# Sixteen-fold positions and remainders written by ScalarE for the routing of a product-key expert layer

## The chip, the cores and the metric

The kernel runs on one core of a Trainium2 chip. The metric is the device time of one execution in microseconds (us); a kernel's time is the median of its runs. The engines are named as the profile names them: PE (TensorE, the matmuls) and PEld (its weight loads), DVE (VectorE), ACT (ScalarE), POOL (GpSimd), SP (the DMA-issuing SyncE).

## The reference

Two layers, each a mixer (attention, convolution and a gated scan) and a channel mixer called PEER, on 512 tokens of width 1024. The change lies in PEER alone:

```python
s1 = jnp.einsum('thd,nd->thn', q[:, :, 0], keys1).astype(jnp.float32)
s2 = jnp.einsum('thd,nd->thn', q[:, :, 1], keys2).astype(jnp.float32)
v1, i1 = lax.top_k(s1, PEER_TOPK)
v2, i2 = lax.top_k(s2, PEER_TOPK)
cand = (v1[..., :, None] + v2[..., None, :]).reshape(T, PEER_HEADS, PEER_TOPK * PEER_TOPK)
sc, ci = lax.top_k(cand, PEER_TOPK)
e1 = jnp.take_along_axis(i1, ci // PEER_TOPK, axis=-1)
e2 = jnp.take_along_axis(i2, ci % PEER_TOPK, axis=-1)
experts = (e1 * PEER_NKEYS + e2).reshape(T, hk)
gates = jax.nn.softmax(sc, axis=-1).reshape(T, hk).astype(xn.dtype)
```

Each token has 8 heads of 16 winners, 128 experts in all; of each expert the layer uses one row of `u` (with a Gelu behind it) and one row of `v`, weighted by the gate.

## The kernel before

Tokens lie in four blocks of 128 (one token to a partition). Three blocks are computed densely: for each of 128 chunks of 128 experts, `hidden` (L639) multiplies the chunk of `u` with the 384 tokens into a PSUM tile `psh` of which there are two; ScalarE makes Gelu of it into `ht` (L645). A chunk of `u` is split in two parts first: ScalarE casts it to `uh` (L630), VectorE subtracts to get `ul` (L631), three buffers each; the matmuls of a chunk need both. For the first 72 chunks `ht` goes to memory as `H` by a DMA that ScalarE's own queue issues (L769). The gates are spread into a dense matrix `G` by `gate_matrix` (L952): four one-hot operations on VectorE for every 16 tokens, matmuls into `psg`, ScalarE copies them to `stg` (L976), and ScalarE's queue issues the DMA to `G` (L977). The fourth block is computed by gathering rows with indirect DMAs (`gathered`, L719), one VectorE step a row; `tick` hands out these steps.

What fills the gate matrix comes from `route` (L878), which runs four times a layer in the order block 0, block 3 (the gathered one), block 1, block 2: "first" to "fourth route" below. It forms 50 candidate sums a head (`cand`), finds the 16 largest and their positions `si` (`top16`), makes the softmax of the gates (an Exp on ScalarE, L898), and then turns a position into a pair of keys. For that it compares each of 128 positions with the 16 starts of the candidate groups (L923, 128x2048 elements of 16 bits), multiplies the result with two tables (L925, L926), sums over the 16 (`total`, L920 and L921), takes the remainder `bi` (L930), compares it with 0 to 15 (L932), multiplies (L933) and sums again. Three transposes on TensorE (`rtr`, L943 to L945) end the first, third and fourth route. In both comparisons the position or remainder is read through `bc(..., [[1, HK], [0, 16]])`: the innermost step of that operand is 0. The tiles `ge`, `pr`, `ci`, `bi` have one buffer each.

The order of the work isn't written out by hand. The program's order gives priorities, and a planner places each instruction on its engine's queue as soon as it takes its inputs to be ready, except where `pin` keeps the order. Each engine then runs its queue in order. A loop over 75 steps (L762) traces one chunk a step, and beside it as much of `route` and `gate_matrix` as keeps the sum of the numbers that their `yield` statements hand out at or below 2.72 a step (L772); rows are gathered from the end of the second route on, 0.8 a step.

Of the kernel before, what the change touches and what calls it, by code (L numbers as in the profile page):

```python
# [10 lines left out]
F16 = mybir.dt.float16  # L11
# [3 lines left out]
OP = mybir.AluOpType  # L15
# [4 lines left out]
P = 128  # L20
# [6 lines left out]
NH = 8  # L27
NK = 16
# [31 lines left out]
def bc(ap, pattern):  # L60
    return bass.AP(tensor=ap.tensor, offset=ap.offset, ap=[ap.ap[0]] + pattern)


class K:
# [813 lines left out]
    def route(self, V12, I12, rp, gate, hk=None, tb=0, idx=None, base=0):  # L878
        nc = self.nc
        cand = rp.tile([P, NH, NCAND], F32, tag="cand", name="cand")  # L880
        v1, v2 = V12[:, 0], V12[:, 1]
        for a in range(5):
            s, n = GRP_START[a], GRP_LEN[a]
            nc.vector.tensor_tensor(cand[:, :, s:s + n], v2[:, :, 0:n], bc(v1[:, :, a:a + 1], [[NK, NH], [0, n]]), op=OP.add)
        s = GRP_START[5]
        nc.vector.tensor_tensor(cand[:, :, s:s + 6].rearrange("p h (a b) -> p h a b", b=2),
                                bc(v1[:, :, 5:8], [[NK, NH], [1, 3], [0, 2]]),
                                bc(v2[:, :, 0:2], [[NK, NH], [0, 3], [1, 2]]), op=OP.add)
        s = GRP_START[8]
        nc.vector.tensor_tensor(cand[:, :, s:s + 8], v1[:, :, 8:16], bc(v2[:, :, 0:1], [[NK, NH], [0, 8]]), op=OP.add)  # L890
        sv = rp.tile([P, NH, NK], F32, tag="sv", name="sv")
        si = rp.tile([P, NH, NK], U32, tag="si", name="si")
        for h in range(NH):
            self.top16(cand[:, h], sv[:, h], si[:, h])
            yield 0.65
        gt = gate.rearrange("p (h k) -> p h k", h=NH)
        nc.vector.tensor_tensor(gt, sv, bc(sv[:, :, 0:1], [[NK, NH], [0, NK]]), op=OP.subtract)
        nc.scalar.activation(gt, gt, AF.Exp)  # L898
        zs = rp.tile([P, NH], F32, tag="zs", name="zs")
        nc.vector.tensor_reduce(zs, gt, axis=AX.X, op=OP.add)  # L900
        nc.vector.reciprocal(zs, zs)
        nc.vector.tensor_tensor(gt, gt, bc(zs, [[1, NH], [0, NK]]), op=OP.mult)

        ci = rp.tile([P, NH, NK], F16, tag="ci", name="ci")
        nc.vector.tensor_copy(ci, si)
        ii = rp.tile([P, 2, NH, NK], F16, tag="ii", name="ii")
        nc.vector.tensor_copy(ii, I12)
        d1 = rp.tile([P, NH, NK], F16, tag="d1", name="d1")
        nc.vector.tensor_copy(d1[:, :, 0:1], ii[:, 0, :, 0:1])
        nc.vector.tensor_tensor(d1[:, :, 1:NK], ii[:, 0, :, 1:NK], ii[:, 0, :, 0:NK - 1], op=OP.subtract)  # L910
        HK = NH * NK
        ge = rp.tile([P, HK, 16], F16, tag="ge", name="ge")
        pr = rp.tile([P, 2, HK, 16], F16, tag="pr", name="pr")
        ex = rp.tile([P, 3, HK], F32, tag="ex", name="ex")
        cib = bc(ci, [[1, HK], [0, 16]])
        yield 2.0

        def total(n, dst):
            for w in (8, 4, 2):
                nc.vector.tensor_tensor(pr[:, 0:n, :, 0:w], pr[:, 0:n, :, 0:w], pr[:, 0:n, :, w:2 * w], op=OP.add)  # L920
            nc.vector.tensor_tensor(dst, pr[:, 0:n, :, 0], pr[:, 0:n, :, 1], op=OP.add)  # L921

        nc.vector.tensor_tensor(ge, cib, bc(self.starts, [[0, HK], [1, 16]]), op=OP.is_ge)  # L923
        hv = lambda t: t.rearrange("p (h k) j -> p h k j", h=NH)
        nc.vector.tensor_tensor(hv(pr[:, 0]), hv(ge), bc(d1, [[NK, NH], [0, NK], [1, 16]]), op=OP.mult)  # L925
        nc.vector.tensor_tensor(pr[:, 1], ge, bc(self.dstart, [[0, HK], [1, 16]]), op=OP.mult)  # L926
        yield 4.6
        total(2, ex[:, 0:2])
        bi = rp.tile([P, HK], F16, tag="bi", name="bi")
        nc.vector.tensor_tensor(bi, ci.rearrange("p h k -> p (h k)"), ex[:, 1], op=OP.subtract)  # L930
        yield 2.6
        nc.vector.tensor_tensor(ge, bc(bi, [[1, HK], [0, 16]]), bc(self.iota16, [[0, HK], [1, 16]]), op=OP.is_equal)  # L932
        nc.vector.tensor_tensor(hv(pr[:, 0]), hv(ge), bc(ii[:, 1], [[NK, NH], [0, NK], [1, 16]]), op=OP.mult)  # L933
        total(1, ex[:, 1:2])
        yield 4.6

        if idx is not None:
            nc.vector.tensor_scalar(ex[:, 0], ex[:, 0], float(NCH), float(base), op0=OP.mult, op1=OP.add)
            nc.vector.tensor_tensor(idx, ex[:, 0], ex[:, 1], op=OP.add)
            return  # L940
        E1, E2, GH, GL = hk
        tr = self.psC.tile([P, 3, P], F32, tag="c", name="rtr2")
        nc.tensor.transpose(tr[:, 0], ex[:, 0], self.ident)  # L943
        nc.tensor.transpose(tr[:, 1], ex[:, 1], self.ident)
        nc.tensor.transpose(tr[:, 2], gate, self.ident)  # L945
        s = slice(tb * P, tb * P + P)
        nc.scalar.copy(E1[:, s], tr[:, 0])
        nc.scalar.copy(E2[:, s], tr[:, 1])
        nc.scalar.activation(GH[:, s], tr[:, 2], AF.Copy, scale=GSCALE)
        nc.vector.scalar_tensor_tensor(GL[:, s], tr[:, 2], GSCALE, GH[:, s], op0=OP.mult, op1=OP.subtract)  # L950
# [97 lines left out]
```

## Time and profile before

| | |
|---|---|
| three runs, median (lowest to highest) | 3073.7 us (3073.36 to 3074.85) |
| the profiled execution | 3068.26 us, of which the span is 3066.5 us |
| granted TensorE clock, mean of the span | 0.994 |

The span runs from the first to the last instruction of the profile; 1.8 us lie around it. The page's busy times are shares of that span. An engine's idle time matters only where the engine that the end waits for stood still with it, so the page is read together with the timeline of single waits.

### The profile page before, as it was taken

The numbers are of one execution on the slowest core, as the hardware profiler recorded it, in microseconds if no ns is written. First come the engines' busy times: TensorE is split into PE (matmuls) and PEld (weight loads), VectorE is DVE, ScalarE is ACT, GpSimd is POOL, SyncE is SP. The second block draws the span as 40 slices with busy tenths as digits, with TensorE's granted clock in tenths as the row PEclk, the third lists the DMA queues.
The fourth block names the chain that finished last, engine by engine and source line by source line (L and its number), as shares of the span: only waits on it lengthen the run. The fifth ranks groups of instructions, "written<-read, shape, count | busy, mean of one in ns | idle before, by whom it ended". The sixth has DMA issues, their size and how long they took to land.

```text
span 3066.5 us, 45595 instructions
## 1 busy us (share of the span) xinstructions
PE 2996.6 (98%) x16742; PEld 2657.9 (87%) x16742; DVE 2470.3 (81%) x5079; ACT 1268.5 (41%) x1874; POOL 739.7 (24%) x543
## 2 busy tenths in 40 slices
PE   8999999999999999999999999999999999999998
PEld 7777889999999998788878788899998999988886
DVE  5777999987778887877766769999878877878777
ACT  5244346556333333333352433465553333323333
POOL 0000000222455544322100000002225555543221
PEclk9999999999999999999999999999999999999999
DMA  4112238799998888999722122478999888889996
GB/s 123 56 45 91 89 122 263 260 316 334 338 333 324 322 325 307 357 338 334 275 76 69 59 72 90 155 246 287 310 343 340 321 326 331 331 306 350 334 344 232
DMA packets 335664, 757.03 MB, mean 247 GB/s; under 512 B 30000, under 2 KB 192208, under 8 KB 331344
## 3 DMA queue, kind: packets, MB, share of 16 engines
q1 hardware_dynamic: 141904, 407.00, 37.1%
q0 software_dynamic: 73728, 268.47, 24.5%
q10 hardware_dynamic: 119808, 78.66, 8.2%
q8 instruction: 131, 2.15, 0.3%
q14 instruction: 93, 0.76, 0.1%
HBM read 673.28 MB, written 80.74 MB: 246 GB/s over the span
## 4 chain that ended last, share of the span: by engine, by line
PE 74%; issue 7%; DVE 7%; POOL 4%; DMA 3%; ACT 3%; ACTq 1%; SPq 0%; POOLq 0%; DVEq 0%
PE pv L77 9%; PE pv L75 9%; PE pv L76 9%; PE psh L75 8%; PE psh L77 8%; PE psh L76 8%; POOL row L715 4%; PE psp L77 2%; PE psp L76 2%; PE psp L75 2%; DMA row<-in_v_rows,idx 2%; PE psq L76 2%; PE psq L77 2%; PE psq L75 2%; PE pst L545 1%
## 5 line engine op out<-in xcount | busy, mean ns | idle before, releaser
L715 POOL DMA_INDIRECT row<-in_u_rows,idx x256 | 390.6, 1526 | 1315.9 <-DVE si L873 669.5
L75 PE MATMUL psh<-ahi,uh 128*128 128x384 f32 x2048 | 694.7, 339 | 10.3 <-ACT ht L645 10.3
L77 PE MATMUL psh<-ahi,ul 128*128 128x384 f32 x2048 | 689.6, 337 | 6.6 <-DVE ul L631 6.6
L76 PE MATMUL psh<-alo,uh 128*128 128x384 f32 x2048 | 688.8, 336 | 0.0
L75 PE MATMUL pv<-vh,wh 128*128 128x512 f32 x1536 | 598.1, 390 | 8.1 <-ACT wh L815 8.1
L77 PE MATMUL pv<-vh,wl 128*128 128x512 f32 x1536 | 601.2, 392 | 0.0
L76 PE MATMUL pv<-vl,wh 128*128 128x512 f32 x1536 | 600.3, 391 | 0.0
L715 POOL DMA_INDIRECT row<-in_v_rows,idx x256 | 331.5, 1295 | 601.5 <-DVE yacc L732 565.7
L630 ACT CAST uh<-uraw 128x1024 fp32r<-128x1024 f32 x288 | 302.5, 1053 | 322.0 <-PE psh L76 156.1
L631 DVE TENSOR_TENSOR ul<-uraw,uh 128x1024 fp32r<-128x1024 f32 x288 | 350.4, 1220 | 99.3 <-ACT uh L630 87.9
L75 PEld LDWEIGHTS psh<-ahi,uh 128*128 128x128 f32 x2048 | 387.0, 189 | 16.4 <-ACT ht L645 12.2
L77 PEld LDWEIGHTS psh<-ahi,ul 128*128 128x128 f32 x2048 | 386.8, 189 | 7.2 <-DVE ul L631 7.2
L76 PEld LDWEIGHTS psh<-alo,uh 128*128 128x128 f32 x2048 | 387.3, 189 | 4.1
L801 DVE TENSOR_TENSOR vl<-vraw,vh 128x1024 fp32r<-128x1024 f32 x256 | 312.6, 1221 | 83.2 <-issue 64.5
L645 ACT ACTIVATE ht<-psh 128x384 f32<-128x384 f32 x256 | 125.3, 489 | 612.4 <-PE psh L77 605.5
L75 PEld LDWEIGHTS pv<-vh,wh 128*128 128x128 f32 x1536 | 288.7, 188 | 67.5 <-ACT wh L815 10.5
L77 PEld LDWEIGHTS pv<-vh,wl 128*128 128x128 f32 x1536 | 289.0, 188 | 62.6 <-DVE wl L801 1.9
L76 PEld LDWEIGHTS pv<-vl,wh 128*128 128x128 f32 x1536 | 289.1, 188 | 59.4 <-DVE vl L801 1.0
L732 DVE SCALAR_TENSOR_TENSOR yacc<-row,wk,yacc 128x1024 f32<-128x1024 f32 x254 | 325.7, 1282 | 10.9 <-DMA row<-in_v_rows,idx 9.3
L723 DVE SCALAR_TENSOR_TENSOR gscr<-row,xg 128x1024 f32<-128x1024 f32 x256 | 312.4, 1220 | 13.2 <-DMA row<-in_u_rows,idx 11.6
L815 ACT CAST wh<-ht 128x384 fp32r<-128x384 f32 x256 | 130.7, 510 | 385.0 <-PE pv L76 229.5
L806 ACT CAST vh<-vraw 128x1024 fp32r<-128x1024 f32 x256 | 268.7, 1050 | 25.3 <-DMA vraw<-in_v_rows 24.5
(285 smaller groups left out, 4451.2 us busy)
## 6 DMA issues: line engine op xcount, KB each, us to landing
uraw<-in_peer_u SPq DMA_DIRECT2D x256, 512.0 KB
vraw<-in_v_rows SPq DMA_DIRECT2D x256, 512.0 KB
G<-stg ACTq DMA_DIRECT2D x48, 1024.0 KB
g<-G SPq DMA_DIRECT2D x32, 1536.0 KB
H<-ht ACTq DMA_DIRECT2D x144, 192.0 KB
ht<-H SPq DMA_DIRECT2D x144, 192.0 KB
wraw<-in_w_in SPq DMA_DIRECT2D x96, 256.0 KB
uraw<-in_peer_w_q SPq DMA_DIRECT2D x32, 512.0 KB
```

Of the source, the lines that this page charges most:

```text
L75: mm(ps, ah, bh, start=first, stop=False)
L76: mm(ps, ah, bl, start=False, stop=False)
L77: mm(ps, al, bh, start=False, stop=last)
L630: pin(nc.scalar.copy(hi, src))
L631: self.last = pin(nc.vector.tensor_tensor(lo, src, hi.bitcast(F32), op=OP.subtract))
L645: pin(nc.scalar.activation(hs[c], ps, AF.Gelu))
L715: nc.gpsimd.indirect_dma_start(out=r, out_offset=None, in_=ins[name], in_offset=bass.IndirectOffsetOnAxis(ap=idx[:, k:k + 1], axis=0))
L723: nc.vector.scalar_tensor_tensor(sc, r, 1.0, xg, op0=OP.mult, op1=OP.mult, accum_out=hd[:, k:k + 1])
L732: nc.vector.scalar_tensor_tensor(yacc, r, wk[:, k:k + 1], yacc, op0=OP.mult, op1=OP.add)
L801: self.last = pin(nc.vector.tensor_tensor(lo, src, hi.bitcast(F32), op=OP.subtract))
L806: pin(nc.scalar.copy(vh[c], vs[c]))
L815: pin(nc.scalar.copy(wh[c], hs[c]))
```

## The change

ScalarE gets two more instructions a route: it copies the 128 positions, and later the 128 remainders, each sixteen times side by side, into the second half of the tile `pr` (2048 elements of 16 bits a partition). Both comparisons on VectorE then read that copy, whose innermost step is 1. The second half of `pr` is free at both places: the product with `dstart` (L926) is written into it behind the first comparison, and has been summed before the second copy. Two `yield` numbers go from 4.6 to 3.6; `ge` and `pr` are declared earlier, and `ci` gets a flat shape.

```diff
-        ci = rp.tile([P, NH, NK], F16, tag="ci", name="ci")
-        nc.vector.tensor_copy(ci, si)
+        HK = NH * NK
+        ge = rp.tile([P, HK, 16], F16, tag="ge", name="ge")
+        pr = rp.tile([P, 2, HK, 16], F16, tag="pr", name="pr")
+        wide = pr[:, 1]
+        nc.scalar.copy(wide, bc(si, [[1, HK], [0, 16]]))
+        ci = rp.tile([P, HK], F16, tag="ci", name="ci")
+        nc.vector.tensor_copy(ci, si.rearrange("p h k -> p (h k)"))
...
-        cib = bc(ci, [[1, HK], [0, 16]])
...
-        nc.vector.tensor_tensor(ge, cib, bc(self.starts, [[0, HK], [1, 16]]), op=OP.is_ge)
+        nc.vector.tensor_tensor(ge, wide, bc(self.starts, [[0, HK], [1, 16]]), op=OP.is_ge)
...
-        yield 4.6
+        yield 3.6
         total(2, ex[:, 0:2])
         bi = rp.tile([P, HK], F16, tag="bi", name="bi")
-        nc.vector.tensor_tensor(bi, ci.rearrange("p h k -> p (h k)"), ex[:, 1], op=OP.subtract)
+        nc.vector.tensor_tensor(bi, ci, ex[:, 1], op=OP.subtract)
+        nc.scalar.copy(wide, bc(bi, [[1, HK], [0, 16]]))
         yield 2.6
-        nc.vector.tensor_tensor(ge, bc(bi, [[1, HK], [0, 16]]), bc(self.iota16, [[0, HK], [1, 16]]), op=OP.is_equal)
+        nc.vector.tensor_tensor(ge, wide, bc(self.iota16, [[0, HK], [1, 16]]), op=OP.is_equal)
...
-        yield 4.6
+        yield 3.6
```

## Rows read from the trace of the kernel before

**Rows 1.** The page: the span, and each engine's busy us (share of the span, instructions).

```profile
span 3066.5 us, 45595 instructions
PE 2996.6 (98%) x16742; PEld 2657.9 (87%) x16742; DVE 2470.3 (81%) x5079; ACT 1268.5 (41%) x1874; POOL 739.7 (24%) x543
```

**Rows 2.** Busy time of each engine over the stretch in which the routing runs, once per layer. Columns: stretch, its length, then busy us (instructions) of PE, PEld, DVE, ACT, POOL, then granted clock, DMA share, GB/s.

```profile
400.00:780.00 380.00, 370.40 (x2603) 363.96 (x2602) 333.82 (x688) 212.68 (x269) 58.57 (x42) 0.99 0.81 271
1920.00:2300.00 380.00, 371.70 (x2619) 364.82 (x2618) 336.52 (x699) 214.20 (x271) 58.81 (x42) 0.99 0.81 269
```

**Rows 3.** Timeline of TensorE in those two stretches, matmuls ahead of which it stood idle (left out: waits under 0.3 us, one of 1.00 us at 428.08, and layer 1's others). Columns: start, length, engine, line, operation, out<-in, and in brackets the idle time before it and what ended it.

```profile
421.08 0.44 PE L77 MATMUL psh<-ahi,ul 128*128 128x384 f32 x1 [3.28 <-DVE ul L631]
441.96 0.33 PE L944 MATMUL rtr<-ident,ex 128*128 128x128 f32 x1 [0.31 <-DVE ex L921]
530.40 0.45 PE L75 MATMUL psh<-ahi,uh 128*128 128x384 f32 x1 [2.85 <-ACT ht L645]
765.89 0.45 PE L75 MATMUL psh<-ahi,uh 128*128 128x384 f32 x1 [1.98 <-ACT ht L645]
2052.56 0.45 PE L75 MATMUL psh<-ahi,uh 128*128 128x384 f32 x1 [2.38 <-ACT ht L645]
```

**Rows 4.** Waits of TensorE over the whole run: its two groups on psh, the tile of the hidden layer's matmuls. Columns: engine, line, what it waited for, us in total, times, longest.

```profile
PE psh L75 <- ACT ht L645: 10.3, 6, 2.8
PE psh L77 <- DVE ul L631: 6.6, 2, 3.3
```

**Rows 5.** Busy time in the 20 us around the wait at 530.40 (columns as in rows 2), for the granted clock; then, from the chain that ended last, a matmul right behind that wait and one 3 us later (start, us, what).

```profile
520.00:540.00 20.00, 17.15 (x90) 16.83 (x89) 20.00 (x48) 7.79 (x10) 1.66 (x1) 0.91 0.80 285
...
531.36 0.32 PE psh L75
534.67 0.17 PE psh L77
```

**Rows 6.** Groups of VectorE instructions by line and shape over the whole run. Columns: line, engine, operation, out<-in, shapes, count, busy us, mean ns of one, idle time before them.

```profile
L923 DVE TENSOR_TENSOR ge<-ci,starts 128x2048 f16<-128x2048 f16 x8 | 18.3, 2283 | 0.0
L932 DVE TENSOR_TENSOR ge<-bi,iota 128x2048 f16<-128x2048 f16 x8 | 18.2, 2278 | 0.0
L926 DVE TENSOR_TENSOR pr<-ge,dstart 128x2048 f16<-128x2048 f16 x8 | 9.7, 1208 | 0.0
```

**Rows 7.** The same view for ScalarE.

```profile
L630 ACT CAST uh<-uraw 128x1024 fp32r<-128x1024 f32 x288 | 302.5, 1053 | 322.0 <-PE psh L76 156.1 <-PE psq L76 82.1 <-PE psg L974 28.2
L976 ACT ACTIVATE stg<-psg 128x512 f32<-128x512 f32 x192 | 186.0, 1121 | 12.2 <-issue 9.9 <-PE psg L974 2.3
L80 ACT CAST wh<-wraw 128x512 fp32r<-128x512 f32 x96 | 57.2, 619 | 44.9 <-DMA wraw<-in_w_in 39.9 <-PE psp L76 4.4
```

**Rows 8.** Timeline of ScalarE (ACT; ACTq is its own queue issuing a DMA) and of VectorE around the third route of layer 0.

```profile
519.79 7.12 ACTq L769 DMA_DIRECT2D H<-ht  x1
526.94 1.28 ACT L898 ACT_TABLE_LOAD   x1 [6.24 <-issue]
528.23 0.31 ACT L898 ACTIVATE gt<-gt 128x128 f32<-128x128 f32 x1
529.86 0.49 ACT L645 ACTIVATE ht<-psh 128x384 f32<-128x384 f32 x1
...
523.78 2.29 DVE L923 TENSOR_TENSOR ge<-ci,starts 128x2048 f16<-128x2048 f16 x1
528.39 1.22 DVE L631 TENSOR_TENSOR ul<-uraw,uh 128x1024 fp32r<-128x1024 f32 x1
```

**Rows 9.** The same place in layer 1, ScalarE.

```profile
2042.41 6.66 ACTq L769 DMA_DIRECT2D H<-ht  x1
2052.01 0.49 ACT L645 ACTIVATE ht<-psh 128x384 f32<-128x384 f32 x1
```

**Rows 10.** First route of layer 0: timeline of ScalarE, then of VectorE.

```profile
436.19 1.05 ACT L630 CAST uh<-uraw 128x1024 fp32r<-128x1024 f32 x1 [2.38 <-PE psh L76]
...
420.94 2.29 DVE L923 TENSOR_TENSOR ge<-ci,starts 128x2048 f16<-128x2048 f16 x1
433.46 1.23 DVE L631 TENSOR_TENSOR ul<-uraw,uh 128x1024 fp32r<-128x1024 f32 x1 [0.75 <-ACT uh L630]
434.60 0.28 DVE L930 TENSOR_TENSOR bi<-ci,ex 128x128 f16<-128x128 f16 x1
434.92 2.29 DVE L932 TENSOR_TENSOR ge<-bi,iota 128x2048 f16<-128x2048 f16 x1
441.54 0.36 DVE L921 TENSOR_TENSOR ex<-pr 128x128 f32<-128x128 f16 x1
```

**Rows 11.** Fourth route of layer 0: timeline of VectorE, then of ScalarE.

```profile
579.12 0.28 DVE L930 TENSOR_TENSOR bi<-ci,ex 128x128 f16<-128x128 f16 x1
...
584.77 0.49 ACT L645 ACTIVATE ht<-psh 128x384 f32<-128x384 f32 x1
586.56 1.05 ACT L630 CAST uh<-uraw 128x1024 fp32r<-128x1024 f32 x1 [1.30 <-PE psh L76]
```

**Rows 12.** VectorE: the last read of the shared tile by the third route of layer 0, and a step of the fourth route behind its last position.

```profile
541.72 0.43 DVE L921 TENSOR_TENSOR ex<-pr 128x128 f32<-128x128 f16 x1
551.96 0.23 DVE L905 CAST ci<-si 128x128 f16<-128x128 uint32 x1
```

**Rows 13.** ScalarE in a stretch with no routing step beside it.

```profile
548.75 1.06 ACT L630 CAST uh<-uraw 128x1024 fp32r<-128x1024 f32 x1 [2.72 <-PE psh L76]
```

More of the change, by code (lines that the diff above doesn't have):

```diff
@@ L910, in route @@
         nc.vector.tensor_tensor(d1[:, :, 1:NK], ii[:, 0, :, 1:NK], ii[:, 0, :, 0:NK - 1], op=OP.subtract)
-        HK = NH * NK
-        ge = rp.tile([P, HK, 16], F16, tag="ge", name="ge")
-        pr = rp.tile([P, 2, HK, 16], F16, tag="pr", name="pr")
         ex = rp.tile([P, 3, HK], F32, tag="ex", name="ex")
-        cib = bc(ci, [[1, HK], [0, 16]])
         yield 2.0
```

## The prediction

> **What bounds the kernel now.** I read the page first: TensorE is busy for 98% of the span, VectorE for 81%, ScalarE for 41% [rows 1]. So VectorE's time is worth something only where TensorE stands still. Next the two stretches that hold the routing, one a layer: in 380 us TensorE is busy for 370.4 and 371.7 us, VectorE for 334 and 337, ScalarE for 213 and 214 [rows 2]. All that the change can win there is the rest of TensorE, 9.6 and 8.3 us, and what a lowered clock costs behind each wait. Then the waits themselves [rows 3]. Those shown of layer 0 are 3.28 us for `ul`, 0.31 us for the end of the first route, 2.85 and 1.98 us for `ht`; the reader is to see that the routing's own products end only the shortest. Summed over the run, TensorE waits on `psh` 10.3 us for ScalarE's `ht` and 6.6 us for VectorE's `ul` [rows 4]. ScalarE, the engine that gets the new work, is the one whose lateness TensorE feels more. Last the clock: in the 20 us around the wait of 2.85 us it was granted at 0.91, and right behind the wait a matmul advances the chain by 0.32 us, 3 us later by 0.17 [rows 5]: the lower of the two levels, 1.2 GHz, after idleness. 9% of 20 us is 1.8 us on top of the wait.
>
> **The change part by part.** *The comparisons.* Sixteen of them (two a route, four routes, two layers) take 2283 and 2278 ns each. The product with `dstart` has the same size and type, and the operands that the comparisons will have, one dense and one 16 values read again and again; it takes 1208 ns [rows 6]. I take that: 1.07 us less each, 17.2 us less VectorE time in all, 8.6 us a layer. On the path to the end this is worth nothing by itself: TensorE's long waits are for `ul` behind the first route's top-16 search, which ends before the first comparison (420.94) [rows 3, 10], and for `ht`. Its bounds are 0 and the 0.31 us a layer of the wait for `rtr`.
>
> *The copies.* Sixteen ScalarE instructions of 2048 elements a partition. No row has that size. The cast between the same memories takes 619 ns for 512 elements and 1053 ns for 1024 [rows 7], 434 ns for each further 512, so 1053 + 2 x 434 = 1.92 us. The strided copy into `stg` takes 1121 ns for 512 [rows 7], which would make 4 x 1121 = 4.48 us; the new copy writes densely, so I take 1.92 and keep 4.48 for the range. ScalarE gets 31 us more in all. The Trainium skill (page "ScalarE: Activation LUTs", section "What ACT_TABLE_LOAD costs") gives 186 ns plus 0.833 ns an element, an estimate of 1.89 us, which leaves the sum as it is.
>
> Away from the routing ScalarE stands idle for 2.72 us ahead of each `uh` cast [rows 13], which hides a copy of 1.92 us whole. Without that cover it would cost up to 1.92 us. Three places are tighter.
>
> *(a) Third route, first copy, both layers.* ScalarE's queue is held for 7.12 us by the issue of an `H` DMA, until 526.94, and only then runs the table load for Exp, Exp at 528.23 and, after another table load, the Gelu into `ht` at 529.86, which releases TensorE at 530.40 [rows 3, 8]. The positions of this route are ready before its first comparison at 523.78, inside the held time [rows 8]. So the copy is queued behind the DMA, beside Exp, in front of that `ht`, and TensorE's wait grows by the copy: 1.92 us. Layer 1 repeats it (6.66 us held, `ht` at 2052.01, wait of 2.38 us) [rows 3, 9]. The clock is already lowered there, so I add nothing for it. Sum 2 x 1.92 = 3.8 us; bounds 0 (queued behind `ht`) and 2 x 4.48 = 9.0.
>
> *(b) First route, second copy.* `bi` is done at 434.88; ScalarE is idle until 436.19; the copy would end at 436.8, the comparison would start 1.9 us later than its 434.92 and last 1.07 us less, so the chain to `rtr` would be 0.8 us longer and the wait at 441.96 with it [rows 3, 10]. Against it: the first comparison ends some 0.7 us earlier in the same route, and VectorE stands idle 0.75 us ahead of the subtraction at 433.46 in front of `bi` [rows 10], so `bi` can come before that subtraction. I take 0; bounds 0 and 2 x 0.8 = 1.6.
>
> *(c) Fourth route, second copy.* `bi` is ready at 579.4. `ht` ends at 585.26 and ScalarE next waits for TensorE until 586.56 [rows 11]: a margin of 1.3 us against 1.92. I take 0; bounds 0 and 2 x 0.6 = 1.2.
>
> *What waits behind a waiting instruction.* A copy that waits for `si` or `bi` holds the `uh` casts, Gelus and DMA issues queued behind it, and TensorE waits for the first two. A comparison that waits for its copy holds the `ul` subtractions and the one-hot operations behind it on VectorE. The copy must also wait until the route before has read `pr` for the last time. The third route does so by 542.15 and the fourth has its positions before 551.96 [rows 12], so this costs nothing; without that margin of nearly 10 us it would hold ScalarE for what was missing.
>
> *The `yield` numbers* fall by 8 a layer, 8 / 2.72 = 2.9 of 75 steps: routing and gate matrices get their priority that much earlier, with their DMAs into `G` on ScalarE's queue, in front of `H` DMAs that the same queue issues. The third route's numbers start at 74.8 before and 70.8 now, that is in step 28 and step 27, so 0.8 of a gathered row more is asked for in these 75 steps, and POOL issues it a step sooner. TensorE's groups of waits on `psh` name no row [rows 4]; I take 0, and the re-sorting that it may cause is in the rivals.
>
> Sum: 3.8 us. Against the profiled execution that is 3068.26 + 3.8 = 3072.1 us; the median of the runs lies 5.4 us above that execution, so I forecast 3073.7 + 3.8 = 3077.5 us.
>
> **The rivals.** *Nothing is seen (3073.7 us):* the copy is queued behind `ht` in (a) too. For it speaks that nothing in the program orders the two; against it, that Exp, whose input comes at nearly the same time, was queued in front of `ht`.
>
> *Faster (3064.9 us):* the copy pushes Exp and its two table loads behind the waiting `ht`. Then `ht` could run at 526.94 in place of 529.86 [rows 8], and the waits of 2.85 and 2.38 us and 1.8 us of clock each would go: 8.8 us. For it: a longer queue at that place is a reason for the planner to take the older `ht` first. Against it: that `ht` must look ready to the planner before Exp does, and in the trace of before it did not.
>
> *Slower (3083 us):* VectorE becomes late behind its new wait. In (a) the copy ends at 526.94 + 1.92 = 528.86 at the earliest, so the comparison starts 5.1 us later than 523.78 and, being 1.07 us shorter, ends 4.0 us later; the subtraction at 528.39 behind it moves to 532.4 and ends at 533.6 [rows 8], 1.3 us after TensorE could go on at 530.40 + 1.92. It decides once that `ul` belongs to the very next chunk. With (b) and (c) in full it is 2 x (1.92 + 1.3 + 0.8 + 0.6) = 9.2 us. Against it: three buffers of `ul`. The Trainium skill (page "ScalarE: Activation LUTs", section "Rules for kernel authors") sends simple elementwise work to VectorE rather than ScalarE, so it speaks against this change. If its exchange were all on one path, 16 x (1.92 - 1.07) = 13.6 us would be lost, 3087.3 us; ScalarE at 41% busy [rows 1] says that most of it is not.
>
> *The comparison isn't shortened (3077.5 us still):* if it stayed at 2.28 us, VectorE would lose what nothing waits for. The row of `dstart` [rows 6] speaks against it.
>
> **How the numbers follow.** Forecast 0.32, nothing seen 0.15, comparison not shortened 0.03, faster 0.22, slower 0.28. About 0.2% (6.1 us) is what a measurement of this kernel can tell from no change; the first three cases lie within it, so the same has 0.50, faster 0.22 and slower 0.28. The range goes from the faster case, rounded down to 3064, to 3084, which takes in the slower case and (a) at the dear copy (3082.7). The prices past both ends are left out.
>
> **What would show it.** After the change the two comparisons should take about 1.2 us, and sixteen ScalarE copies about 1.9 us. At the held `H` DMA of each layer the copy should stand in front of the `ht` that releases TensorE, and that wait should be 4.8 and 4.3 us. The wait for `rtr` should stay near 0.3 us. I am wrong if the waits on `ul` multiply in the routing stretches, if the held place is reordered, or if TensorE's idle time changes outside these stretches.

## The result and the profile after

The changed kernel takes 3095.39 us (median of 6 runs, 3091.6 to 3100.69), the kernel before 3074.27 us on the same chip (6 runs, 3068.8 to 3077.99): +21.1 us, a ratio of 1.0070 with a 95% interval of 1.0057 to 1.0083. That is past the upper end of the range.

The profiled execution of the changed kernel took 3100.69 us, 5.3 above its median; that of the kernel before (3068.26) lay 6.0 below the median of 3074.27. So the two profiles stand 32.4 us apart where the medians stand 21.1. Below, places are read from the profiles and sizes from the medians.

First the page, beside [rows 1], and the groups of the new and changed instructions, beside [rows 6] (count, busy us, mean ns of one, idle time before them).

```profile
span 3098.9 us, 45600 instructions
PE 3006.6 (97%) x16742; PEld 2665.2 (86%) x16742; DVE 2454.0 (79%) x5079; ACT 1295.6 (42%) x1890; POOL 746.8 (24%) x543
```

```profile
L932 ACT COPY pr<-bi 128x2048 f16<-128x2048 f16 x8 | 15.2, 1899 | 12.4 <-DVE bi L931 12.0 <-ACT ht L645 0.4
L908 ACT CAST pr<-si 128x2048 f16<-128x2048 uint32 x8 | 15.1, 1892 | 12.0 <-DVE si L876 9.6 <-issue 2.4
L924 DVE TENSOR_TENSOR ge<-pr,starts 128x2048 f16<-128x2048 f16 x8 | 9.8, 1223 | 8.6 <-ACT pr L908 8.6
L934 DVE TENSOR_TENSOR ge<-pr,iota 128x2048 f16<-128x2048 f16 x8 | 9.7, 1213 | 2.3 <-ACT pr L932 1.5 <-issue 0.8
```

The prices are those forecast: comparisons of 1.21 to 1.22 us, copies of 1.89 to 1.90 (forecast 1.92). VectorE is busy 16.3 us less, ScalarE 27.1 us more, and TensorE does the same 16742 matmuls. The time is lost in where things stand. Layer 0's routing stretch, cut at the start of chunks 0, 25, 49 and 75 of `psh`, before and after (columns as in [rows 2]):

```profile
403.81:536.24 132.43, 124.99 (x868) 122.29 (x867) 131.12 (x380) 77.16 (x96) 4.84 (x4) 0.97 0.64 210
536.24:652.15 115.91, 115.73 (x836) 114.31 (x836) 109.82 (x189) 64.25 (x82) 25.11 (x17) 1.00 0.84 283
652.15:780.08 127.93, 125.95 (x888) 124.33 (x886) 89.63 (x100) 70.67 (x90) 28.62 (x21) 0.99 0.96 327
```

```profile
405.28:532.35 127.07, 122.94 (x869) 120.65 (x867) 109.31 (x313) 79.89 (x97) 0.00 (x0) 0.99 0.65 205
532.35:662.80 130.45, 120.79 (x836) 117.11 (x836) 113.10 (x242) 76.56 (x92) 30.43 (x21) 0.97 0.83 276
662.80:796.82 134.02, 127.64 (x885) 125.08 (x885) 101.25 (x116) 69.82 (x88) 33.40 (x22) 0.97 0.92 315
```

The first third gains 5.4 us (the waits of 1.00 and 2.85 us of [rows 3] are gone), the second loses 14.5 and the third 6.1, with the clock granted at 0.97 in place of 1.00 and 0.99. VectorE did 313 instructions in the first third where it did 380: the routing has slid to the right. Layer 1's stretch, before and after:

```profile
1926.43:2299.91 373.48, 365.18 (x2586) 359.43 (x2585) 330.64 (x667) 212.10 (x268) 58.81 (x42) 0.99 0.82 272
```

```profile
1943.21:2333.71 390.50, 372.51 (x2586) 363.47 (x2585) 323.61 (x669) 226.04 (x276) 59.70 (x43) 0.98 0.80 267
```

That is 17.0 us more, and 15.3 in layer 0: together 32.3 of the 32.4 us by which the profiles differ, so next to nothing is lost outside these stretches. TensorE's waits over 1 us in layer 0's (same view as [rows 3]) are new ones, but for the 3.28 us for `ul` behind the first route's search, which stay:

```profile
558.92 0.69 PE L77 MATMUL psh<-ahi,ul 128*128 128x384 f32 x1 [5.26 <-DVE ul L631]
578.50 0.33 PE L946 MATMUL rtr<-ident,ex 128*128 128x128 f32 x1 [1.73 <-DVE ex L922]
656.42 0.44 PE L75 MATMUL psh<-ahi,uh 128*128 128x384 f32 x1 [2.15 <-ACT ht L645]
664.48 0.45 PE L75 MATMUL psh<-ahi,uh 128*128 128x384 f32 x1 [1.16 <-ACT uh L630]
781.49 0.69 PE L75 MATMUL psh<-ahi,uh 128*128 128x384 f32 x1 [4.43 <-ACT ht L645]
```

Layer 1 has the waits for `ul` (3.12 us) and for `rtr` (1.74) again; at its end two waits for `ht`, of 1.92 and 1.99 us, stand in place of the 4.43.

*The wait at 558.92.* The timelines of ScalarE (first row), VectorE and POOL around the second route:

```profile
516.29 1.89 ACT L908 CAST pr<-si 128x2048 f16<-128x2048 uint32 x1
...
518.22 1.23 DVE L924 TENSOR_TENSOR ge<-pr,starts 128x2048 f16<-128x2048 f16 x1 [2.08 <-ACT pr L908]
541.20 0.27 DVE L941 TENSOR_TENSOR idx<-ex 128x128 int32<-128x128 f32 x1
547.32 1.23 DVE L723 SCALAR_TENSOR_TENSOR gscr<-row,xg 128x1024 f32<-128x1024 f32 x1 [1.73 <-DMA row<-in_u_rows,idx]
552.91 1.23 DVE L723 SCALAR_TENSOR_TENSOR gscr<-row,xg 128x1024 f32<-128x1024 f32 x1 [3.60 <-DMA row<-in_u_rows,idx]
557.65 1.22 DVE L631 TENSOR_TENSOR ul<-uraw,uh 128x1024 fp32r<-128x1024 f32 x1
...
542.41 1.09 POOL L715 DMA_INDIRECT row<-in_u_rows,idx  x1 [360.34 <-DVE sv L875]
543.81 2.16 POOL L715 DMA_INDIRECT row<-in_u_rows,idx  x1 [0.30 <-issue]
```

The second route's first copy stands on ScalarE behind the copies into `stg` of the first route's gate matrix, though its positions were ready at 487.40, so its comparison runs at 518.22, where before it ran at 486.45, and `idx` comes at 541.20 in place of 514.67. Before, the first row step ran at 550.43, 36 us behind `idx`; now VectorE comes to it at 545.6 (547.32 less the 1.73 of waiting), 4 us behind `idx`, while the first row takes 4.9 us from its issue at 542.41. VectorE waits for two rows in turn, and `ul` with it.

*The wait at 781.49.* SyncE's queue at the end of the stretch, before and after:

```profile
758.34 0.33 SPq L627 DMA_DIRECT2D uraw<-in_peer_u  x1
768.94 0.33 SPq L791 DMA_DIRECT2D g<-G  x1
```

```profile
761.23 0.61 SPq L627 DMA_DIRECT2D uraw<-in_peer_u  x1
769.18 0.33 SPq L791 DMA_DIRECT2D g<-G  x1
769.60 1.08 SPq L627 DMA_DIRECT2D uraw<-in_peer_u  x2
...
780.00 1.04 ACT L630 CAST uh<-uraw 128x1024 fp32r<-128x1024 f32 x1 [8.58 <-DMA uraw<-in_peer_u]
```

The last stage's first load of `g` waits for the last `G` DMA. Before it was queued behind the stretch's 76th `uraw` load, now behind the 73rd, so five loads (74 to 78) stand behind that wait in place of two, and ScalarE waits 8.58 us for one.

### The profile page after: what moved, and what is told of

It is laid out like the page before. It is cut to its first block, busy times and chain, and to the rows that moved or that the text cites. A ratio compares the mean times of both kernels' runs of the same rounds, so it can differ in the third digit from the quotient of the medians.

```text
span 3098.9 us, 45600 instructions
## 1 busy us (share of the span) xinstructions
PE 3006.6 (97%) x16742; PEld 2665.2 (86%) x16742; DVE 2454.0 (79%) x5079; ACT 1295.6 (42%) x1890; POOL 746.8 (24%) x543
## 5 line engine op out<-in xcount | busy, mean ns | idle before, releaser
L77 PE MATMUL psh<-ahi,ul 128*128 128x384 f32 x2048 | 694.6, 339 | 15.3 <-DVE ul L631 15.2
L631 DVE TENSOR_TENSOR ul<-uraw,uh 128x1024 fp32r<-128x1024 f32 x288 | 350.3, 1220 | 127.0 <-ACT uh L630 115.9
L732 DVE SCALAR_TENSOR_TENSOR yacc<-row,wk,yacc 128x1024 f32<-128x1024 f32 x254 | 325.8, 1283 | 14.5 <-DMA row<-in_v_rows,idx 13.1
```

What stands on the lines that cost most here:

```text
L77: mm(ps, al, bh, start=False, stop=last)
L631: self.last = pin(nc.vector.tensor_tensor(lo, src, hi.bitcast(F32), op=OP.subtract))
L732: nc.vector.scalar_tensor_tensor(yacc, r, wk[:, k:k + 1], yacc, op0=OP.mult, op1=OP.add)
```

## The experiments

Differences are median against median of the kernel before on the same chip. "Loads behind" means that the last stage's first loads (`vraw`, `g`) are queued behind the last `uraw` of the stretch. The ratio and the two medians don't agree to the microsecond everywhere: e9's 1.0046 is 14 us, its medians give 11.6. Each interval reaches some 3 to 6 us to either side, so a difference between two rows of the table is known to about 5 us only (an estimate from these intervals).

| label | copies in routes | numbers | else | median us | against before | ratio (95% interval) |
|---|---|---|---|---|---|---|
| change | all | 3.6 | | 3095.39 | +21.1 | 1.0070 (1.0057 to 1.0083) |
| e1 | all | 3.6 | copies planned first | 3101.07 | +26.5 | 1.0087 (1.0072 to 1.0102) |
| e2 | 1, 3, 4 | 3.6 | | 3082.88 | +8.3 | 1.0029 (1.0019 to 1.0038) |
| e3 | 2 | 3.6 | | 3095.88 | +21.3 | 1.0065 (1.0049 to 1.0082) |
| e4 | none | 3.6 | | 3090.26 | +15.7 | 1.0049 (1.0036 to 1.0062) |
| e5 | none | 3.6 | loads behind | 3077.09 | +2.8 | 1.0006 (0.9997 to 1.0015) |
| e6 | none | 4.6 | loads behind | 3072.86 | -1.5 | 0.9993 (0.9982 to 1.0005) |
| e7 | all | 4.6 | | 3075.11 | +0.8 | 1.0003 (0.9991 to 1.0015) |
| e8 | all | 3.6 | loads behind | 3091.65 | +17.3 | 1.0053 (1.0039 to 1.0067) |
| e9 | all | 3.6 | loads behind, rows later | 3085.79 | +11.6 | 1.0046 (1.0031 to 1.0061) |
| e10 | 1, 3, 4 | 3.6 | loads behind | 3078.24 | +4.0 | 1.0013 (1.0004 to 1.0022) |
| e11 | all | 4.6 | loads behind | 3073.10 | -1.1 | 1.0000 (0.9989 to 1.0011) |
| e12 | all | 4.6 | rows sooner | 3082.13 | +7.9 | 1.0026 (1.0017 to 1.0036) |
| e13 | all | 3.6 in 1, 2 | loads behind | 3078.04 | +3.5 | 1.0015 (1.0003 to 1.0028) |
| e14 | all | 3.6 in 3, 4 | loads behind | 3077.19 | +2.6 | 1.0010 (1.0000 to 1.0020) |
| e15 | all | 5.6 | loads behind | 3080.63 | +6.1 | 1.0015 (1.0005 to 1.0025) |
| e16 | all | 3.6 in 1, 2 | loads behind, rows later | 3073.07 | -1.5 | 0.9998 (0.9987 to 1.0008) |
| e17 | 1, 2, 3 | 3.6 | loads behind | 3088.85 | +15.3 | 1.0053 (1.0033 to 1.0073) |
| e18 | all | 4.6 | loads behind, `H` from SyncE | 3141.80 | +68.3 | 1.0217 (1.0201 to 1.0233) |

**Is the copy's place the price?** (e1 to e4) The first theory was that the late second route alone makes the loss.

```diff
+        with self.tc.high_priority():                       # e1, both copies
             nc.scalar.copy(wide, bc(si, [[1, HK], [0, 16]]))
...
+        wide1 = idx is None                                 # e2; e3: idx is not None
+        if wide1:
             nc.scalar.copy(wide, bc(si, [[1, HK], [0, 16]]))
-        nc.vector.tensor_tensor(ge, wide, bc(self.starts, [[0, HK], [1, 16]]), op=OP.is_ge)
+        nc.vector.tensor_tensor(ge, wide if wide1 else bc(ci, [[1, HK], [0, 16]]), bc(self.starts, [[0, HK], [1, 16]]), op=OP.is_ge)
```

e1:

> The changed kernel, but both copies of each route are given to the planner ahead of everything else that is ready (in the changed kernel the first copy of the second route stands on ScalarE behind the copies into stg of the first route's gate matrix). The copies are as many and as long. Theory (place in the queue): the second route is on time again and the loss goes: 0 to +6 us against the kernel before, VectorE's empty stretches of 4 to 6 us around 500 to 518 us are gone. Rival (ScalarE's time in the copies is the price): +15 to +22 us as in the changed kernel. Rival (any re-sorting does it): no sign foretold, 10 us either way.

e2:

> The changed kernel, but the second route (the one whose rows are gathered) compares as before, without copies; the other three routes keep theirs, and the smaller yield numbers stay. Theory (the late copy of the second route holds the gathering and all that follows): 0 to +6 us against the kernel before. Rival (ScalarE's time): three quarters of the loss stays, +14 to +17 us. Rival (the yield numbers): the whole loss stays, about +21 us.

e3:

> The changed kernel with copies in the second route alone; the other three compare as before, without copies. Theory: nearly the whole loss, +14 to +21 us against the kernel before. Rival (ScalarE's time): a quarter of it, about +5 us. Rival (the yield numbers): the whole loss, about +21 us, so this run parts the theory from it only together with the run that has the yield numbers alone.

e4, the kernel before with `yield 4.6` twice replaced by `yield 3.6`:

> The kernel before with the two smaller yield numbers alone: no copies. Theory: -3 to +4 us against the kernel before, the second route ends in the same place. Rival (the yield numbers re-sort the stream): about +21 us.

The theory falls with e4, which loses 15.7 us without a copy. e1 brings `idx` back to 518.41 and loses more than the change, but in another place: layer 0's second third is 118.2 us long (130.5 in the change, 115.9 before), its first 143.1 (127.1 and 132.4). So it says little about what the late route costs. e2 (+8.3) lies between its cases, and e3 (+21.3) fits the theory and the numbers alike. What e1 lost, in the timelines of ScalarE and TensorE:

```profile
524.29 1.90 ACT L909 CAST pr<-si 128x2048 f16<-128x2048 uint32 x1 [4.76 <-DVE si L876]
526.10 2.81 ACT L980 ACTIVATE stg<-psg 128x512 f32<-128x512 f32 x3
528.72 0.51 ACT L645 ACTIVATE ht<-psh 128x384 f32<-128x384 f32 x1
532.02 1.05 ACT L630 CAST uh<-uraw 128x1024 fp32r<-128x1024 f32 x1 [2.79 <-issue]
...
533.12 0.69 PE L75 MATMUL psh<-ahi,uh 128*128 128x384 f32 x1 [6.76 <-ACT uh L630]
```

A copy planned early waits 4.76 us at the head of ScalarE's queue, with `stg`, `ht` and `uh` behind it; TensorE waits 6.76.

**The place of g, and a square of copies and numbers** (e5 to e8, e11).

```diff
+            with tc.issue_after(self.lastu.ins):    # the last uraw load traced
-            for i in range(3):
-                at(load_v, i)
-                at(load_g, i)
+                for i in range(3):
+                    at(load_v, i)
+                    at(load_g, i)
```

e5:

> The kernel before with the two smaller yield numbers alone (measured +15.7 us), and the first loads of the last stage (three vraw, g and what goes with them) kept on SyncE's queue behind the last uraw load of the stretch. Theory (with the smaller numbers the load of g, which waits for the last gate matrix, comes to stand in front of five uraw loads in place of two, and TensorE runs out of chunks at its end: 5 to 6 us a layer): +2 to +6 us against the kernel before, the wait of 3.8 us at the end of the stretch is gone. Rival (the re-sorting earlier in the stretch is the price): +13 to +17 us, as without the edit.

e6:

> The kernel before with that one edit: the first loads of the last stage behind the last uraw load. Theory: -3 to +1 us, since g stands in front of two uraw loads only there, and the wait at 765.89 us is for a Gelu behind a held DMA issue, not for uraw. Rival (later vraw and g loads starve the start of the last stage): +4 to +10 us.

e7:

> The changed kernel with the two yield numbers back at 4.6: the copies alone. Theory of two terms (numbers 10 to 15 us, late copies the rest): +6 to +11 us against the kernel before, and g stands as in the kernel before. Rival (the copies are the whole price, the numbers only another way to the same re-sorting): +18 to +22 us. Rival (the numbers are the whole price): -2 to +3 us.

e8:

> The changed kernel with the first loads of the last stage behind the last uraw load. Theory: the 4.43 us wait at its stretch's end goes, 8 to 12 us less than the changed kernel: +9 to +13 us against the kernel before. Rival (the place of g decides nothing): +19 to +22 us.

e11:

> The copies with the old yield numbers and the last stage's first loads behind the last uraw load: the fourth corner of a square of copies and numbers, all with these loads in one place. Theory: -3 to +2 us against the kernel before, so the two parts of the change cost nothing and 3 us alone and 17 us together. Rival (the copies cost by themselves, hidden by chance in the run with the old numbers): +5 us or more.

e4 has the same wait as the change at the end of the stretch (TensorE, ScalarE):

```profile
774.92 0.69 PE L75 MATMUL psh<-ahi,uh 128*128 128x384 f32 x1 [3.84 <-ACT ht L645]
...
773.43 1.04 ACT L630 CAST uh<-uraw 128x1024 fp32r<-128x1024 f32 x1 [9.37 <-DMA uraw<-in_peer_u]
```

With the loads behind it is gone, and 12.9 of the 15.7 us with it (e4 to e5): shown for the numbers alone. In the change the same edit takes back only 3.8 us (e8, between its two cases), and the intervals of the two runs overlap. e5, e6 and e11 came out as their theories said. e7 decides against the theories in which the copies bring 6 us or more, the one of two terms too: +0.8 us, with an interval that ends at +4.6 (e11's ends at +3.4), though `idx` is nearly as late (538.73). Its third case, the numbers as the whole price, has the right size, but e4 alone is 5.4 us short of the change. Near 0 doesn't mean that nothing moved: in e7's profile layer 0's first third is 127.0 us long (132.4 before) and its second 121.4 (115.9), so what the copies gain in one place they lose in the next, and nothing in the change makes the two equal. With these loads in one place in all four corners, copies cost 0.4 us (e6 to e11), numbers 4.3 (e6 to e5), and both together 18.8 (e6 to e8), so about 14 us lie in their meeting. Without that edit the same square reads 0.8 (e7), 15.7 (e4) and 21.1 (the change), with 4.6 in the meeting, which these intervals can't tell from 0. So the place of `g` and the meeting take part of the same time, and how much each is given depends on which is taken away first.

**Rows ahead of their landing** (e9, e10, e12). VectorE's queue as built, where uN is the subtraction `ul` of the N-th chunk (here counted from 1), r a row step, a one-hot step `oha`, C1 and C2 the comparisons:

```
change  u28 u29 IDX  u30rr C1  u31r u32r u33 u34r C2  u35r u36raa u37ra u38 u39ra u40r
e7      u28 IDX  u29 C1  u30r u31r u32r u33r C2  u34 u35r u36r u37r C1  u38ara u39a u40r
e9      u28 u29 IDX  u30 C1  u31r u32r u33r u34r C2  u35r u36r u37aara u38 u39ra u40r
e12     u28 IDX  u29r C1 r u30r u31r u32 u33r u34r C2  u35r u36r u37 u38ara u39ra u40r
```

```diff
-                    if live:                        # e9, on top of e8
-                        tick(RATE[0])
+                    if live and c > live + 2:
+                        tick(0.86)
...
-                            live = True
+                            live = c
...
                             live = True             # e12, on top of e7
+                            tick(1.6)
```

e9:

> The changed kernel with the last stage's first loads behind the last uraw load (measured +17.3 us against the kernel before) and, in addition, the gathered rows asked for from three steps later on, 0.86 a step in place of 0.8. In its queue VectorE then has no row step between idx and the third route's first comparison; without the edit two stand there in a row, and VectorE waits 1.73 and 3.60 us for rows not yet landed with ul behind them. Theory (small numbers and late copies together bring row steps in front of their rows): the waits for ul of 3.78 and 2.94 us go, and what the clock loses with them; +5 to +10 us against the kernel before. Rival (late routes crowd the gate matrices of the last two blocks, rows or not): +14 to +18 us.

e10:

> The changed kernel without copies in the second route, with the last stage's first loads behind the last uraw load. idx is then written in chunk 22's place of VectorE's queue, 7 chunks ahead of the first row step. Theory (it is the second route's late copy that meets the small numbers): +1 to +5 us against the kernel before. Rival (copies in any route meet them): +10 to +17 us.

e12:

> The copies with the old yield numbers (measured +0.8 us against the kernel before), but the gathered rows start with 1.6 rows in the very step in which idx is written, so that in VectorE's queue a row step stands ahead of the third route's first comparison and two between two ul. Theory (row steps that come ahead of their rows hold ul and the comparison): TensorE waits 3 to 6 us a layer for ul near 550 and 2080 us, +6 to +12 us against the kernel before. Rival (the rows' time of arrival decides nothing): -1 to +3 us.

e12 makes the wait in a kernel that had none of it: 7.1 us slower than e7, the size expected, with this at TensorE in layer 0, shorter than expected (layer 1 has no such wait; there the longest new one is 2.89 us, 1.53 in e7, ahead of a `psg` matmul behind VectorE's one-hot step):

```profile
553.16 0.69 PE L77 MATMUL psh<-ahi,ul 128*128 128x384 f32 x1 [2.56 <-DVE ul L631]
```

e9 takes the row steps away and e8's wait of 3.78 us goes, but the kernel gains only 5.7 us by the medians (2 by the ratios), which these runs barely tell from nothing, and lands between the two expectations (by the ratio at the rival's lower end): the rows are one part, and as far as these runs can tell not the larger. e10 (+4.0, as expected) bears out that the second route's late copy has to be there for the loss.

**Which numbers, and whether they have a direction** (e13 to e16).

```diff
-        yield 3.6
+        yield 3.6 if tb == 0 else 4.6   # both; e13, e16: first and second route
+        yield 4.6 if tb == 0 else 3.6   # e14: third and fourth
+        yield 5.6                       # e15
```

e13:

> The copies with the last stage's first loads behind the last uraw load, and the smaller numbers in the first two routes alone (4.6 kept in the third and fourth). Two row steps then stand together behind idx, as in the changed kernel. Theory (the first two routes' numbers set when the rows and the third route start, and these meet the late idx): +10 to +16 us against the kernel before. Rival (the third and fourth routes' numbers do it by crowding the last gate matrices): 0 to +5 us.

e14:

> The same with the smaller numbers in the third and fourth routes alone; the row steps stand as in the run with the old numbers. Theory: 0 to +5 us against the kernel before. Rival: +10 to +16 us.

e15:

> The copies with the last stage's first loads behind the last uraw load, and the two numbers at 5.6 in place of 3.6 or 4.6: routing and gate matrices are traced later. Theory (numbers that are too small trace the routing earlier than idx and rows come): -4 to +3 us against the kernel before. Rival (4.6 is where the stream happens to fall well, each step away from it costs): +8 us or more.

e16 has the rows of e9 as well:

> The smaller numbers in the first two routes alone, loads behind, and the gathered rows asked for from three steps later on, 0.86 a step: no row step ahead of the third route's first comparison. Theory if the rows are all that the first two routes' numbers touch: 0 to +4 us against the kernel before. If it is the third route's chain that comes early against its copies as well (TensorE waits 2 to 3 us for rtr): +6 to +12 us.

e13 (+3.5) came out as the rival said and e14 (+2.6) as the theory, so each of the two is right once and wrong once: neither half makes the loss. e13 has the wait for rows in full (TensorE, layer 0), and still costs only 3.5 us; e16 takes it away and gains 5.0.

```profile
556.53 0.69 PE L77 MATMUL psh<-ahi,ul 128*128 128x384 f32 x1 [4.07 <-DVE ul L631]
```

The two sizes add up: by the medians, later rows are worth 5.7 us (e8 to e9) and 5.0 (e13 to e16); the last two routes' small numbers, on top of small ones in the first two, 13.8 us (e13 to e8) and 13.1 (e16 to e9), but only 3.7 without them (e11 to e14). e15 (+6.1) lies between its cases. It pays at another end, in each layer's first wait of the last stage:

```profile
790.39 0.80 PE L75 MATMUL pv<-vh,wh 128*128 128x512 f32 x1 [9.33 <-ACT wh L815]
2318.05 0.80 PE L75 MATMUL pv<-vh,wh 128*128 128x512 f32 x1 [10.07 <-ACT wh L815]
```

There the gate matrices end so late that the load of `g` goes out at 781.29 (768.94 before). With the copies there, 4.6 lies between two losses.

**The rest, and a faster version** (e17, e18). Where e8 loses against e13, the fourth route's Exp, copy and table loads follow a held `H` issue. In the change this is the row that the prediction looked for in the third route, though here copies into `stg`, a cast and a Gelu still run between the issue and Exp (timeline of ScalarE):

```profile
646.15 6.13 ACTq L769 DMA_DIRECT2D H<-ht  x1
656.39 1.28 ACT L898 ACT_TABLE_LOAD   x1
657.91 1.90 ACT L908 CAST pr<-si 128x2048 f16<-128x2048 uint32 x1
```

```diff
+        wide1 = tb != 2                                       # e17, on top of e8; used as in e2
...
-                        nc.scalar.dma_start(H[c], hs.pop(c))  # e18, on top of e11
+                        nc.sync.dma_start(H[c], hs.pop(c))
```

e17:

> The changed kernel with the last stage's first loads behind the last uraw load (measured +17.3 us against the kernel before), and without copies in the fourth route, which compares as before. There Exp, the first copy and two table loads (4.7 us) stand together on ScalarE behind an H DMA issue that holds it for 4.58 us, in front of Gelu and uh; without the copy it is 2.9 us. Theory (these 1.9 us and what the clock loses are part of the rest): 3 to 8 us less, +9 to +14 us against the kernel before. Rival (the rest lies in the gate matrices being denser, not in this place): +16 to +19 us.

e18:

> The copies with the old yield numbers, the last stage's first loads behind the last uraw load (measured -1 us against the kernel before), and the H DMAs issued from SyncE's queue, so that no H issue can hold ScalarE. Theory (ScalarE's held issues are what Gelu, uh and the copies wait for): TensorE's waits for ht in the routing stretches go, -3 to -9 us against the kernel before. Rival (an H issue behind which uraw loads stand on SyncE's queue makes these late): +3 to +15 us, with waits for uh behind uraw.

e17 gains 2 us by the medians and none by the ratios. It lies between its cases, and its interval (+10 to +22 us) holds both. The wait moves: with the comparisons back at 2.28 us, `ul` is late behind the second of them, and TensorE waits at 663.00, where it had waited for `uh` (timeline of VectorE, then TensorE):

```profile
659.33 2.29 DVE L938 TENSOR_TENSOR ge<-bi,iota 128x2048 f16<-128x2048 f16 x1
661.74 1.22 DVE L631 TENSOR_TENSOR ul<-uraw,uh 128x1024 fp32r<-128x1024 f32 x1
...
663.00 0.44 PE L77 MATMUL psh<-ahi,ul 128*128 128x384 f32 x1 [2.89 <-DVE ul L631]
```

So taking the copy away there buys little, because the longer comparisons make a wait in the same place; whether the copy is a part of the cause stays undecided. e18 is slower than either of its cases: on SyncE's queue each `H` issue waits for its Gelu with `uraw` loads behind it, and ScalarE's waits for `uraw` go from 22.2 us in e11 (9.3 in the kernel before) to this:

```profile
ACT uh L630 <- DMA uraw<-in_peer_u: 213.6, 79, 9.0
```

No version beats the kernel before by more than the interval allows; the nearest are e6 (0.9993) and e16 (0.9998).

## Why the prediction was wrong

*The step that failed is the `yield` numbers, priced at 0.* The prediction worked out that routing, gate matrices and rows are asked for some three steps earlier, then took 0 because TensorE's groups of waits in the trace of before name no row [rows 4]. Alone they cost 15.7 us (e4), and with them back at 4.6 the change costs 0.8 (e7). The prediction looked at ScalarE's queue for the earlier `G` DMAs and at POOL's for the rows, and not at SyncE's, on which the load that waits for the last `G` DMA moved ahead of three more `uraw` loads: 12.9 us of the 15.7 (e5). And a wait that isn't there says nothing of the margin. The margin of the rows could be read: `idx` at 514.67, first row step at 550.43. The late copy used up 26.5 of these 36 us and the earlier row step 4.8, which left 4, less than the first row takes.

*Comparisons: right.* 1.21 to 1.22 us, and worth nothing on the path: 16.3 us less VectorE time bought no time in e7. The Trainium skill's price of the copy (page "ScalarE: Activation LUTs", section "What ACT_TABLE_LOAD costs", an estimate of 1.89 us by its formula) agrees with the measured 1.89 and 1.90 us. The Trainium skill (same page, section "Rules for kernel authors") sends simple elementwise work to VectorE. The 13.6 us that the prediction worked out for the exchange, were it all on one path, don't show: e7 and e11 have +0.8 and -1.1 us.

*Copies (a): the price of 1.92 us was right, its place was wrong.* The sum put 3.8 us on the held `H` issue of the third route. That place dissolved: the waits of 2.85 and 2.38 us [rows 3] are gone in the change, which the prediction had named as a sign of error ("if the held place is reordered"; another of its signs came too: TensorE's waits on `psh` for `ul` went from 6.6 to 15.2 us), and the same row turned up 126 us later in the fourth route. The prediction bound each copy to where its input was ready in the old trace, and asked what stands behind it. What stands ahead counts as much: in the second route, which the prediction didn't look at, the older copies into `stg` kept the copy back. The copies alone cost +0.8 us in e7, whose interval holds 3.8, and -1.1 in e11, whose interval ends at +3.4. The cover of 2.72 us ahead of each `uh` cast was read off a single cast [rows 13], beside which VectorE was in the fourth route's search; over all 288 casts ScalarE's idle time is 322.0 us [rows 7], 1.1 us each.

*(b) and (c): near 0, as taken.* The wait for `rtr` at the first route's end is 0.69 us in both layers against 0.31 [rows 3], within the bound of 0.8. The fourth route's is 0.78 us in layer 0. The waits of 1.73 and 1.74 us at the third route's end had no term in the prediction.

*The rivals.* "Nothing is seen" would have held for the copies alone. "Slower", VectorE late behind its new wait with `ul` behind it, has the right sign, but VectorE's waits for the copies are 10.1 us in the run (8.6 and 1.5), and TensorE's wait comes from rows. The range of 3064 to 3084 left out prices past both ends, and none of its cases let two parts of the change meet.

*What stays open.* From the change to the kernel before, the steps are 3.8 us for the place of `g` (to e8), 5.7 for the rows (to e9) and 13.1 for the last two routes' small numbers (to e16, -1.5). Only the last is well clear of the noise of some 5 us, and in another order the sizes would be others. The last is shown as a size and not as a mechanism: in the profiles e8 against e13 loses 6.5 us between chunks 25 and 49 of layer 0 (130.46 against 123.97) and 2.7 in the same place of layer 1 (125.25 against 122.51), where the fourth route starts amid gate matrices, and e17 leaves open what the copy there has to do with it. That one step of the planner does it and not the sum of several small displacements wasn't tried.

## What to carry to other kernels

Where a planner orders the work, a change of weights or priorities is a change of every queue: list what each queue holds that waits for something late (here one load of `g`), and count what comes to stand behind it. Read margins, not only waits: the time from a result to its first use in the old trace is what a new delay may use up. Try the parts of a change alone and together; here each alone, with one load fixed, cost at most 4.3 us, and both together 18.8, each known to about 5 us.

## What the runs showed of the hardware beyond that

A gathered row can take much longer than its issue suggests: the second row of layer 0 was issued at 543.81 for 2.16 us and its step began at 552.91, 9.1 us after the issue began, with the DMA engines 81% busy between 540 and 560 us. What decides how long was not tried.
